# Splitting the normed tokens out of PSUM, and feeding a gated projection from stored high and low parts

## The chip, the cores and the metric

The kernel runs on one core of a Trainium2 chip. The metric is the device time in microseconds (us) of one execution. TensorE (PE in the profile; its weight loads are PEld) multiplies, VectorE (DVE), ScalarE (ACT) and GpSimd (POOL) work elementwise, and SyncE (SP) issues most of the DMAs. SBUF is the working memory of all engines; PSUM is where TensorE's results land.

## The reference

One layer of a hybrid decoder trunk, 2048 tokens of 1024 channels, all in float32. What is computed, cut to what matters here:

```
h  = rmsnorm(x, norm_pre_mix)                 # 2048 x 1024
z  = h @ w_in                                 # split into g_u, g_v | q, k, v, gate | q_mem
A  = gelu(g_u) * (tril(w_s) @ rmsnorm(gelu(g_v)) + b_s)      # spatial gating, chunks of 128 tokens, 6 groups
B  = forgetting attention over q, k, v, 6 heads x 64: softmax(q k / 8 + c[t] - c[s]) v
C  = attention of q_mem to 256 memory rows, 4 heads x 64
x  = x + rmsnorm(concat(A, B, C) @ w_out)
x  = x + rmsnorm(relu(rmsnorm(x) @ w_ff1)^2 @ w_ff2)         # 1024 -> 4096 -> 1024
```

## The kernel before

**Two parts for each number.** TensorE multiplies in a format with fewer bits than float32 (fp32r in the profile). So a number a is split into a high part (a copy or cast to fp32r) and a low part (a minus the high part), and a product is three matmuls: high by high, high by low, low by high (`mm3`, lines 201 to 203). Making the two parts costs one ACT or DVE cast and one DVE or POOL subtraction for each tile.

**Blocks and their sums.** Large products use seven products of 2 x 2 blocks in place of eight. For this the transposed normed tokens are wanted as four blocks (channels by halves, token tiles by pairs) and four sums t1 to t4 of the blocks, all of them in high and low parts.

**The stages**, in the order of the program:

- Rows stage 0 (`rows_stage(0, h)`, about 8 to 69 us): 1024 tokens, as four pairs of token tiles of 128 x 1024. For a tile: load x (line 409), the sum of squares by an ACT Square whose own output is not used ("junk", line 395), square root (207) and reciprocal (208), then one DVE operation `h = x * r * gain` (397), eight TensorE transposes into two PSUM banks (427). Each bank is one block of 128 x 512, called `pt`. Each block is copied by ACT to SBUF (`hb`, line 428), then split from there (`halves`, lines 400 and 401): high by ACT, low by DVE. Four DVE subtractions on `hb` give the sums (433 to 436), which are split too, with their low parts on POOL. One DMA of 1 MB stores `hb` of the pair to a DRAM scratch tensor `bq` (439). Then the projection to values and forget gates: 48 matmuls `va` per pair.
- Columns stage 0 (to about 149 us): queries and keys of these 1024 tokens, from the blocks and sums.
- Rows stage 1 and columns stage 1 for the other 1024 tokens (about 149 to 205, and 205 to 305 us). A tile scheduler sets the order of instructions in these four stages by its own estimates.
- Token mixing (about 305 to 842 us): the two attentions and the spatial gating with its projection `g_u, g_v`, interleaved. The order on every engine is written by a planner (`Plan`): it simulates the engines with a cost for each operation and with counts of free buffers, and takes the foremost ready operation by a due time `at`. For the gating, each of 16 token tiles is loaded back from `bq` into `hr` (line 1047, two buffers), split again into `ht` (ACT, line 1060; POOL, line 1063; two buffers) and multiplied as `ga`.
- Out-projection and the first feed-forward product, then the second feed-forward product (842 us to the end).

SP works its DMAs off in the order in which they stand in the program, and an issue that waits for something holds up those behind it. The PSUM pools of the first four stages are `ps_x` (4 banks), `ps_y` (2; used by the columns stages) and `ps_c` (2; the transposes). The normed tile `h` has one SBUF buffer for the first tile of a pair and one for the second (in pair 1 of stage 0 both tiles use the first). x tiles have two buffers.

Of the kernel before, what the change touches and what calls it, by code (L numbers as in the profile page):

```python
# [16 lines left out]
P = 128  # L17
S = 2048
D = 1024
# [21 lines left out]
def f32(ap):  # L41
    return ap.bitcast(F32)
# [9 lines left out]
class Plan:  # L52
    """Orders operations for engines that run in order: each engine in turn takes, of the operations whose inputs are
    there and whose buffers are free, the one that is foremost by 'at'. slots: how many buffers there are by name."""

    # until another engine sees a result
    SEEN = {"PE": 0.21, "ACT": 0.18, "DVE": 0.18, "Pool": 0.18, "SP": 0.1}
    # until the same engine does
# [71 lines left out]
def kernel(  # L130
# [46 lines left out]
    bq_d = [dram(f"bq{s}", [4, P, 4, KT // 2, P]) for s in range(NSB)]  # L177
# [40 lines left out]
    # Products of large matrices multiply 2 x 2 blocks by Winograd's seven products:  # L218
    # of blocks a11 .. a22 and b11 .. b22, with s and t sums of the blocks,
    #   c11 = p1 + p2, u2 = p1 + p6, u4 = u2 + p5, c12 = u4 + p3, c21 = u2 + p7 - p4, c22 = u4 + p7  # L220

    def combos(pl, src, nm, dst, q):
        """Blocks of 256 transposed tokens (channels by halves, tokens by tiles) and their sums, to dst"""
# [77 lines left out]
    def columns(nm, weights, h, kp, cp, px, py, emit, before):  # L301
        """Two column tiles of weights by 1024 tokens; emit(f, n, c): what becomes of columns f, tokens n"""
# [53 lines left out]
    # in-projection, 1024 tokens at a time: by rows the values and forget gates, by columns the queries and keys  # L356
# [26 lines left out]
    def rows_stage(s, h):  # L383
        """1024 tokens: norm, transposes, sums of blocks to h; values and forget gates"""
        with ExitStack() as st:
# [19 lines left out]
            def load_pair_of_tiles(q):  # L405
# [9 lines left out]
                # blocks b12, b11, b21, b22: channels by halves, tokens by tiles  # L415
                b = rp.tile([P, 4, KH, P], F32, name=f"hb{s}_{q}", tag="raw")
                own = [xc.tile([P, KH, P], F32R, name=f"b12{w}_{s}_{q}", tag=f"b12{w}") for w in range(2)]
                hl = {m: [t[:, q] for t in h[m]] for m in h}
                hl[0] = own
                for e, ms in enumerate(((1, 2), (0, 3))):  # L420
                    hn = (xd if e and s + q != 1 else xa).tile([P, D], F32, name=f"h{tiles[e]}", tag="h")
                    norm(tiles[e], xt[e], b[:, ms[0] : ms[1] + 1 : ms[1] - ms[0]].rearrange("p m k t -> p m (k t)"), hn)
                    for half, m in enumerate(ms):
                        pt = ps_c.tile([P, KH, P], F32, name=f"pt{s}_{q}_{m}", tag="c")
                        for k in range(KH):
                            kc = half * KH + k
                            nc.tensor.transpose(pt[:, k, :], hn[:, kc * P : (kc + 1) * P], ident)
                        (nc.scalar.copy if m in (0, 1, 2, 3) else nc.vector.tensor_copy)(b[:, m], pt)
                for m in (1, 2, 0, 3):
                    halves(m, hl[m], b[:, m])  # L430
                t1, t3, t2, t4 = [xb.tile([P, KH, P], F32, name=f"t{m}_{s}_{q}", tag="b") for m in (5, 7, 6, 4)]
                es = [nc.vector] * 4
                es[1].tensor_tensor(out=t3, in0=b[:, 3], in1=b[:, 0], op=ALU.subtract)
                es[0].tensor_tensor(out=t1, in0=b[:, 0], in1=b[:, 1], op=ALU.subtract)
                es[2].tensor_tensor(out=t2, in0=b[:, 3], in1=t1, op=ALU.subtract)
                es[3].tensor_tensor(out=t4, in0=b[:, 2], in1=t2, op=ALU.subtract)
                for m, t in ((7, t3), (6, t2), (4, t4), (5, t1)):
                    halves(m, hl[m], t)
                nc.sync.dma_start(bq_d[s][q], b)
                return tiles, hl  # L440

            def rows(tiles, hl):
                """Values and forget gates of two token tiles"""
# [17 lines left out]
    def forget_sums():  # L461
        """c_d: running sums of log sigmoid(gate)"""
        # log sigmoid(z) = min(z, 0) - log1p(exp(-|z|)), log1p(e) = 2 atanh(e / (2 + e))
# [41 lines left out]
    def out_sums(kk, sc):  # L505
        """Sums of the blocks of the out-projection's weights, rows kk of both halves"""
# [14 lines left out]
    def memory_keys(w1p, cp_):  # L521
        """Keys and values of the memory"""
# [48 lines left out]
    def gating_weights(hl, rows):  # L571
        """Of the spatial gating's projection the next rows"""
# [61 lines left out]
    def out_block(m, kk):  # L634
        """Rows kk of an operand of the out-projection's product m"""
# [8 lines left out]
    # token mixing  # L644
    with ExitStack() as st:
# [10 lines left out]
        # causal mask, as what is subtracted from a diagonal block of scores  # L656
# [8 lines left out]
        # weights of the spatial gating and of its projection; of the former the lower triangles, keys on partitions  # L665
# [16 lines left out]
        def chain(name, new):  # L682
            """Operations of one name start in the order in which they are given"""
# [4 lines left out]
        def load_pair(name, tag, hi, lo, half, cols):  # L688
            """[hi; lo] of 64 channels on 128 partitions"""
# [7 lines left out]
        def context(u, kt, half, b, pv, recip, at):  # L697
            """Sum of the halves of pv, over the row sums, to rows half*64.. of context tile kt"""
# [30 lines left out]
        def products(u, nk, first, source, values, vfree, pfree, deps, at):  # L729
            """Transposes the probabilities of 512 queries and multiplies them with the values; returns where the products are"""  # L730
# [864 lines left out]
```

## Time and profile before

| | us |
|---|---|
| runs | 2294.2, 2300.56, 2306.31 (median 2300.56) |
| profiled execution: span | 2300.8 |
| PE busy | 2179.4 (95%) |
| DVE busy | 1626.0 (71%) |
| ACT busy | 1356.0 (59%) |
| POOL busy | 1041.5 (45%) |

The profile's page states no time for the profiled execution other than its span, 2300.8 us from the first to the last instruction; that is the time the sums below are made against, and it lies 0.2 us from the median of the runs. In the profile a row of a group reads: line, engine, operation, result <- operands, shapes, count, then busy time, mean duration of one in ns, and the idle time of the engine just ahead of them with what ended it. A row of the timeline reads: start, duration, engine, line, operation. A row of a table of windows gives the busy time of each engine in a stretch of the span, the TensorE clock that was granted as a share of the full clock (PEclk), and the share of time and the rate of the DMA engines.

### The profile page before, as it was taken

The page shows a single profiled execution, that of the slowest core. Times are in us where ns is not written, and L with a number is a line of the kernel's source. Part 1 is how long each engine was busy: PE and PEld are TensorE (multiplying, and loading weights), DVE is VectorE, ACT ScalarE, POOL GpSimd, SP SyncE. Part 2 cuts the span into 40 slices and gives each one's busy share as a digit, 9 for nine tenths or more (in the row PEclk, how much of TensorE's full clock was granted, in tenths as well). Part 3 has the DMA queues.
Part 4 walks back from the last instruction along what each step waited for, and adds up shares of the span by engine and source line. Part 5 has one row for each costly group of instructions (what it writes and reads, how often), then busy time and mean ns, then how long its engine had stood idle before and what let it go on. Part 6 is the DMA issues. An engine that isn't in the chain of part 4 may idle for free. (4 is left out here: it accounts for less than half of the span.)

```text
span 2300.8 us, 33009 instructions
## 1 busy us (share of the span) xinstructions
PE 2179.4 (95%) x10468; PEld 1830.4 (80%) x10468; DVE 1626.0 (71%) x3137; ACT 1356.0 (59%) x2929; POOL 1041.5 (45%) x1073
## 2 busy tenths in 40 slices
PE   7999989999999979998999999999999999999996
PEld 7777768888888857776888878888788888888874
DVE  8779656777877798995333363333579988998899
ACT  6455567778877776675555575555654443344343
POOL 5445432362636155553333333353365435544564
PEclk9999999999999999999999999999999999999998
DMA  6775685365453355786333353343132212221245
GB/s 221 255 243 174 213 225 131 90 161 133 117 147 98 87 156 209 262 298 217 121 113 113 110 187 113 113 149 113 59 116 92 92 56 92 92 92 57 91 157 182
DMA packets 220715, 330.62 MB, mean 144 GB/s; under 512 B 23014, under 2 KB 139628, under 8 KB 219516
## 3 DMA queue, kind: packets, MB, share of 16 engines
q1 hardware_dynamic: 208252, 287.55, 40.2%
q0 software_dynamic: 12288, 40.95, 4.8%
q8 instruction: 83, 1.36, 0.2%
q14 instruction: 92, 0.75, 0.1%
HBM read 218.20 MB, written 110.23 MB: 143 GB/s over the span
## 5 line engine op out<-in xcount | busy, mean ns | idle before, releaser
L195 DVE TENSOR_TENSOR w_f<-sf,w_f 128x512 fp32r<-128x512 f32 x128 | 92.9, 726 | 176.0 <-ACT w_f L193 171.6
L201 PE MATMUL gx<-w,hc 128*128 128x512 f32 x512 | 200.0, 394 | 14.7 <-DVE ya L1478 11.1
L203 PE MATMUL fxf<-h,w_f 128*128 128x512 f32 x512 | 200.4, 391 | 6.4 <-DVE w_f L195 6.4
L202 PE MATMUL fxf<-h,w_f 128*128 128x512 f32 x512 | 200.0, 391 | 1.2 <-DVE h L195 1.2
L201 PE MATMUL fxf<-h,w_f 128*128 128x512 f32 x512 | 200.2, 391 | 0.9 <-ACT w_f L193 0.5
L202 PE MATMUL gx<-w,hc 128*128 128x512 f32 x512 | 200.3, 391 | 0.0
L193 ACT ACTIVATE hc<-hs 128x256 fp32r<-128x256 f32 x256 | 105.7, 414 | 156.2 <-PE gx L202 62.1
L203 PE MATMUL gx<-w,hc 128*128 128x512 f32 x512 | 196.8, 391 | 0.0
L748 DVE TENSOR_TENSOR pl<-pt,ph 128x512 fp32r<-128x512 f32 x240 | 140.8, 605 | 46.8 <-ACT ph L744 43.1
L195 DVE TENSOR_TENSOR hc<-hs,hc 128x256 fp32r<-128x256 f32 x256 | 146.9, 577 | 36.1 <-PE gx L203 33.8
L860 ACT ACTIVATE p<-p,nm 128x512 f32<-128x512 f32 (+2 forms) x240 | 156.9, 658 | 24.9 <-DVE nm L850 24.5
L1478 DVE TENSOR_TENSOR ya<-gx,ya 128x512 f32<-128x512 f32 x232 | 155.8, 678 | 4.6 <-PE gx L203 4.3
L744 ACT CAST ph<-pt 128x512 fp32r<-128x512 f32 x240 | 120.6, 523 | 63.8 <-PE pt L740 54.4
L193 ACT ACTIVATE hc<-hr 128x256 fp32r<-128x256 f32 x192 | 79.3, 416 | 126.8 <-PE gx L202 83.3
L195 DVE TENSOR_TENSOR w_f<-wrf,w_f 128x512 fp32r<-128x512 f32 x96 | 70.0, 729 | 110.8 <-ACT w_f L193 110.8
L193 ACT ACTIVATE w_f<-sf 128x512 fp32r<-128x512 f32 x128 | 80.8, 631 | 106.3 <-PE fxf L202 61.8
L831 DVE CUSTOM_DVE_ANT_0 p<-s,cb 128x512 f32<-128x512 f32 (+2 forms) x216 | 124.6, 592 | 18.5 <-PE pt L740 10.2
L1459 POOL TENSOR_TENSOR hs<-hr 128x256 f32<-128x256 f32 x64 | 59.6, 932 | 167.9 <-DVE hc L195 75.2
L201 PEld LDWEIGHTS gx<-w,hc 128*128 128x128 f32 x512 | 96.7, 189 | 38.5 <-DVE ya L1478 14.5
L740 PE MATMUL pt<-ident,p 128*128 128x128 f32 x816 | 124.1, 278 | 2.7 <-ACT p L860 2.6
L810 POOL TENSOR_TENSOR cm<-cb,cmask 128x128 f32<-128x128 f32 x96 | 44.9, 468 | 175.9 <-DVE mx L831 141.1
L740 PEld LDWEIGHTS pt<-ident,p 128*128 128x128 f32 x816 | 102.7, 144 | 23.2 <-ACT p L860 2.9
(380 smaller groups left out, 7089.6 us busy)
## 6 DMA issues: line engine op xcount, KB each, us to landing
wrf<-in_w_ff_dram SPq DMA_DIRECT2D x64, 512.0 KB, 4.8
hid<-c_f SPq DMA_DIRECT2D x128, 256.0 KB, 2.2
hr<-hid SPq DMA_DIRECT2D x64, 512.0 KB, 4.1
w2r<-in_w_ff_dram SPq DMA_DIRECT2D x16, 1024.0 KB, 6.6
b<-ty POOLq DMA_DIRECT2D x56, 256.0 KB, 3.7
xt<-in_x_dram SPq DMA_DIRECT2D x16, 512.0 KB, 4.1
bq<-hb SPq DMA_DIRECT2D x8, 1024.0 KB, 5.3
hr<-bq SPq DMA_DIRECT2D x32, 256.0 KB, 5.0
```

The costliest lines, as they stand in the source:

```text
L193: a = nc.scalar.activation(hi, src, AF.Copy, scale=scale)
L195: return a, (eng or nc.vector).tensor_tensor(out=lo, in0=src, in1=f32(hi), op=ALU.subtract)
L201: nc.tensor.matmul(acc, lh, rh, start=first, stop=False, skip_group_check=more)
L202: nc.tensor.matmul(acc, lh, rl, start=False, stop=False, skip_group_check=more)
L203: nc.tensor.matmul(acc, ll, rh, start=False, stop=last, skip_group_check=more)
L740: nc.tensor.transpose(pt[:, a * P : (a + 1) * P], source(a, j), ident)
L744: nc.scalar.copy(hi[:, a0 * P :], tiles["pt", j][:, a0 * P :])
L748: nc.vector.tensor_tensor(out=lo[:, a0 * P :], in0=tiles["pt", j][:, a0 * P :], in1=f32(tiles["hi", j][:, a0 * P :]), op=ALU.subtract,)
L831: nc.vector.tensor_tensor_reduce(out=pr[:, cols], in0=t["s", a, c][:, cols], in1=sub, scale=1.0, scalar=-3.0e38, op0=ALU.subtract, op1=ALU ...
L860: nc.scalar.activation(pr, pr, AF.Exp, bias=t["nm", a], accum_out=t["rs"][:, a, c : c + 1])
L1459: nc.gpsimd.tensor_tensor(out=t[7], in0=a11, in1=a21, op=ALU.subtract)
L1478: nc.vector.tensor_tensor(out=y, in0=a, in1=y, op=ALU.add)
```

## The change

In the rows stages:

- The blocks are split straight from the PSUM banks of the transposes: the high part (ACT) and the low part (DVE) read `pt`. Only blocks 0 and 1 are still copied to SBUF, as second operands of the sums; the sums' first operand is `pt`. So eight DVE operations of a pair that read two SBUF operands now read one PSUM and one SBUF operand, with t2's and t4's second operand still a sum in SBUF, and two of four ACT copies go.
- A bank is held until its last reader is done; the banks of the pair's second tile come from `ps_y`.
- The Square's unused output goes to `h` itself, no longer to `hb`.
- The DRAM scratch `bq` holds high and low parts in place of the values: eight stores of 256 KB for a pair in place of one of 1 MB.

In token mixing, a token tile's high and low parts are loaded ready, two loads of 512 KB in place of two of 256 KB, and the ACT cast and the POOL subtraction go. What the planner orders there is simulated anew, with these operations gone, and with the load of a tile waiting for one of two `ht` buffers (there were two `hr` buffers ahead of them).

```diff
-    bq_d = [dram(f"bq{s}", [4, P, 4, KT // 2, P]) for s in range(NSB)]
+    bq_d = [dram(f"bq{s}", [4, 2, 2, P, 2, KT // 2, P]) for s in range(NSB)]
...
-                b = rp.tile([P, 4, KH, P], F32, name=f"hb{s}_{q}", tag="raw")
+                b = rp.tile([P, 2, KH, P], F32, name=f"hb{s}_{q}", tag="raw")
...
+                pts = {}
                 for e, ms in enumerate(((1, 2), (0, 3))):
                     hn = (xd if e and s + q != 1 else xa).tile([P, D], F32, name=f"h{tiles[e]}", tag="h")
-                    norm(tiles[e], xt[e], b[:, ms[0] : ms[1] + 1 : ms[1] - ms[0]].rearrange("p m k t -> p m (k t)"), hn)
+                    norm(tiles[e], xt[e], hn.rearrange("p (m c) -> p m c", m=2), hn)
                     for half, m in enumerate(ms):
-                        pt = ps_c.tile([P, KH, P], F32, name=f"pt{s}_{q}_{m}", tag="c")
+                        bank, tag = (ps_y, "y") if e else (ps_c, "c")
+                        pt = pts[m] = bank.tile([P, KH, P], F32, name=f"pt{s}_{q}_{m}", tag=tag)
                         for k in range(KH):
                             kc = half * KH + k
                             nc.tensor.transpose(pt[:, k, :], hn[:, kc * P : (kc + 1) * P], ident)
-                        (nc.scalar.copy if m in (0, 1, 2, 3) else nc.vector.tensor_copy)(b[:, m], pt)
-                for m in (1, 2, 0, 3):
-                    halves(m, hl[m], b[:, m])
+                        if m in (0, 1):
+                            nc.scalar.copy(b[:, m], pt)
+                        halves(m, hl[m], pt)
+                        for w in range(2):
+                            nc.sync.dma_start(bq_d[s][q, e, w, :, half], f32(hl[m][w]))
...
-                es[1].tensor_tensor(out=t3, in0=b[:, 3], in1=b[:, 0], op=ALU.subtract)
-                es[0].tensor_tensor(out=t1, in0=b[:, 0], in1=b[:, 1], op=ALU.subtract)
-                es[2].tensor_tensor(out=t2, in0=b[:, 3], in1=t1, op=ALU.subtract)
-                es[3].tensor_tensor(out=t4, in0=b[:, 2], in1=t2, op=ALU.subtract)
+                nc.vector.tensor_tensor(out=t3, in0=pts[3], in1=b[:, 0], op=ALU.subtract)
+                nc.vector.tensor_tensor(out=t1, in0=pts[0], in1=b[:, 1], op=ALU.subtract)
+                nc.vector.tensor_tensor(out=t2, in0=pts[3], in1=t1, op=ALU.subtract)
+                nc.vector.tensor_tensor(out=t4, in0=pts[2], in1=t2, op=ALU.subtract)
...
-                nc.sync.dma_start(bq_d[s][q], b)
...
-                        t["hr", i] = xp.tile([P, D], F32, name=f"hr{i}", tag="x").rearrange("p (k t) -> p k t", k=KT)
-                        for k2 in range(2):
-                            nc.sync.dma_start(
-                                t["hr", i][:, k2 * KH : (k2 + 1) * KH], bq_d[s][q][:, ((1, 2), (0, 3))[e][k2]]
-                            )
...
-                    ld = chain("ld2", op("SP", 1.0, tokens, [], at - 8.0, takes=["hr"], late=4.0))
...
-                        o = chain("th", op("ACT", 0.478, thigh, [ld], at - 4.0, takes=["ht"] * (k2 == 0)))
-                        ht.append(op("Pool", 1.225, tlow, [o], at - 4.0, frees=["hr"] * k2))
+                        for w in range(2):
+                            t["ht", i, w] = hp.tile([P, KT, P], F32R, name=f"ht{w}_{i}", tag=f"ht{w}")
+                            load(
+                                t["ht", i, w].rearrange("p k t -> p (k t)"),
+                                bq_d[s][q, e, w].rearrange("p h k t -> p (h k t)"),
+                            )
+                    ht.append(chain("ld2", op("SP", 1.0, tokens, [], at - 8.0, takes=["ht"], late=4.0)))
```

Two places show how the change moves instructions. In the rows below `pt` are the transposes' banks, `hb` the SBUF copies of blocks, `hc` and `b` the high and low parts, `xt` the x tiles, `h` the normed tiles, `ss` the sums of squares, `r` the root, `vs` the values.

First place: ACT in rows stage 0 from the transposes of pair 1 on. Before:

```order
L428 COPY hb_1_330<-pt_1_1_340 128x512
L395 ACTIVATE hb_2_460,ss_464<-xt_456 128x1024
L428 COPY hb_1_330<-pt_1_2_346 128x512
L400 CAST hc_1_202<-hb_1_330 128x512
L207 ACTIVATE r<-ss_464,eps_t 128x1
L193 ACTIVATE vs_451<-va_426 128x6x64
L400 CAST hc_2_198<-hb_1_330 128x512
L428 COPY hb_1_330<-pt_1_0_359 128x512
L428 COPY hb_1_330<-pt_1_3_365 128x512
L400 CAST b_0_1_331<-hb_1_330 128x512
L395 ACTIVATE hb_2_460,ss_483<-xt_457 128x2x512
L400 CAST hc_3_190<-hb_1_330 128x512
```

And now:

```order
L431 COPY hb_1_335<-pt_1_1_345 128x512
L400 CAST hc_1_202<-pt_1_1_345 128x512
L400 CAST hc_2_198<-pt_1_2_355 128x512
L395 ACTIVATE h_364,ss_365<-xt_332 128x1024
L207 ACTIVATE r<-ss_365,eps_t 128x1
L193 ACTIVATE vs_566<-va_541 128x6x64
L431 COPY hb_1_335<-pt_1_0_371 128x512
L400 CAST b_0_1_336<-pt_1_0_371 128x512
L400 CAST hc_3_190<-pt_1_3_381 128x512
L395 ACTIVATE h_473,ss_474<-xt_466 128x1024
L395 ACTIVATE h_499,ss_500<-xt_467 128x1024
L207 ACTIVATE r<-ss_474,eps_t 128x1
```

Two copies are gone. The Squares of pair 2 (`xt_456` and `xt_457` before, `xt_466` and `xt_467` now) stood among the copies and casts of pair 1; now both stand behind pair 1's last cast, and the Square of pair 1's own second tile (`xt_332`) stands between the casts of the first and those of the second.

Second place: SP at the start of token mixing, down to the queries of the second block of 512 (`q_0_2`). `cb`, `q`, `k` and `v` belong to the forgetting attention, `gvn`, `gws` and `wur` are weights of the gating. Before:

```order
L797 DMA cb_0_3118<-c_d 128x512
L1047 DMA hr_3104<-bq_91 128x512 x2
L187 DMA v_0_3120<-v_d 128x4x128
L797 DMA cb_1_3125<-c_d 128x512
L187 DMA q_0_1_3107<-qhi_67 64x512 x2
L187 DMA q_0_1_3110<-qlo_70 64x512 x2
...
L187 DMA v_1_3127<-v_d 128x4x128
L985 DMA gvn<-in_gmlp_v_norm_dram 128x384
L984 DMA gws<-in_gmlp_w_s_dram 128x6x128
L187 DMA q_0_2_3156<-qhi_67 64x512 x2
L187 DMA q_0_2_3159<-qlo_70 64x512
```

And now:

```order
L187 DMA v_0_3161<-v_d 128x4x128
L799 DMA cb_1_3166<-c_d 128x512
L187 DMA v_1_3168<-v_d 128x4x128
L799 DMA cb_2_3277<-c_d 128x512
L187 DMA q_0_1_3148<-qhi_67 64x512 x2
...
L987 DMA gvn<-in_gmlp_v_norm_dram 128x384
L187 DMA q_0_2_3195<-qhi_67 64x512
L187 DMA ht_0_3144<-bq_91 128x1024
L187 DMA ht_0_3146<-bq_91 128x1024
L986 DMA gws<-in_gmlp_w_s_dram 128x6x128
L187 DMA q_0_2_3195<-qhi_67 64x512
```

The first token tile's load stood second in the stage and was 512 KB; now it is 1 MB and stands behind the first block's queries and keys, in the midst of the second block's queries, and one more `cb` stands ahead.

More of the change, by code (lines that the diff above doesn't have):

```diff
@@ L427, in load_pair_of_tiles @@
                             nc.tensor.transpose(pt[:, k, :], hn[:, kc * P : (kc + 1) * P], ident)
-                        (nc.scalar.copy if m in (0, 1, 2, 3) else nc.vector.tensor_copy)(b[:, m], pt)
-                for m in (1, 2, 0, 3):
-                    halves(m, hl[m], b[:, m])
-                t1, t3, t2, t4 = [xb.tile([P, KH, P], F32, name=f"t{m}_{s}_{q}", tag="b") for m in (5, 7, 6, 4)]
-                es = [nc.vector] * 4
-                es[1].tensor_tensor(out=t3, in0=b[:, 3], in1=b[:, 0], op=ALU.subtract)
-                es[0].tensor_tensor(out=t1, in0=b[:, 0], in1=b[:, 1], op=ALU.subtract)
-                es[2].tensor_tensor(out=t2, in0=b[:, 3], in1=t1, op=ALU.subtract)
-                es[3].tensor_tensor(out=t4, in0=b[:, 2], in1=t2, op=ALU.subtract)
+                        if m in (0, 1):
[3 more added lines that the diff above has]
+                            nc.sync.dma_start(bq_d[s][q, e, w, :, half], f32(hl[m][w]))
+                t1, t3, t2, t4 = [xb.tile([P, KH, P], F32, name=f"t{m}_{s}_{q}", tag="b") for m in (5, 7, 6, 4)]
+                nc.vector.tensor_tensor(out=t3, in0=pts[3], in1=b[:, 0], op=ALU.subtract)
+                nc.vector.tensor_tensor(out=t1, in0=pts[0], in1=b[:, 1], op=ALU.subtract)
+                nc.vector.tensor_tensor(out=t2, in0=pts[3], in1=t1, op=ALU.subtract)
+                nc.vector.tensor_tensor(out=t4, in0=pts[2], in1=t2, op=ALU.subtract)
                 for m, t in ((7, t3), (6, t2), (4, t4), (5, t1)):
                     halves(m, hl[m], t)
-                nc.sync.dma_start(bq_d[s][q], b)
                 return tiles, hl
@@ L1044, in tokens @@
                         s, e, q = i // 8, i // 4 % 2, i % 4
-                        t["hr", i] = xp.tile([P, D], F32, name=f"hr{i}", tag="x").rearrange("p (k t) -> p k t", k=KT)
-                        for k2 in range(2):
-                            nc.sync.dma_start(
-                                t["hr", i][:, k2 * KH : (k2 + 1) * KH], bq_d[s][q][:, ((1, 2), (0, 3))[e][k2]]
-                            )
-                    ld = chain("ld2", op("SP", 1.0, tokens, [], at - 8.0, takes=["hr"], late=4.0))
-                    for k2 in range(2):
-                        ks = slice(k2 * KH, (k2 + 1) * KH)
-                        def thigh(i=i, k2=k2, ks=ks):
-                            for w in range(2):
-                                t["ht", i, w, k2] = hp.tile(
-                                    [P, KH, P], F32R, name=f"ht{w}_{k2}_{i}", tag=f"ht{w}_{k2}"
-                                )
-                            nc.scalar.copy(t["ht", i, 0, k2], t["hr", i][:, ks])
-                        def tlow(i=i, k2=k2, ks=ks):
-                            nc.gpsimd.tensor_tensor(
-                                out=t["ht", i, 1, k2], in0=t["hr", i][:, ks], in1=f32(t["ht", i, 0, k2]), op=ALU.subtract
-                            )
-                        o = chain("th", op("ACT", 0.478, thigh, [ld], at - 4.0, takes=["ht"] * (k2 == 0)))
-                        ht.append(op("Pool", 1.225, tlow, [o], at - 4.0, frees=["hr"] * k2))
+                        for w in range(2):
[3 more added lines that the diff above has]
+                                bq_d[s][q, e, w].rearrange("p h k t -> p (h k t)"),
+                            )
+                    ht.append(chain("ld2", op("SP", 1.0, tokens, [], at - 8.0, takes=["ht"], late=4.0)))
                     for w in range(2):
@@ L1075, in project @@
                             mm3(
-                                t["ga", w][:, :DG], t["ht", i, 0, k // 4][:, k % 4, :], t["ht", i, 1, k // 4][:, k % 4, :],
+                                t["ga", w][:, :DG], t["ht", i, 0][:, k, :], t["ht", i, 1][:, k, :],
                                 wg[k][0][:, cs], wg[k][1][:, cs], k == 0, k == KT - 1,
```

## The prediction

> **What bounds the kernel now.** I read the table of windows first, to see which engine is full in which stage, then DVE's groups by shape in the stages that change, then what PE waits for there.
>
> ```profile
> 8.00:69.00 61.00, 51.98 (x256) 48.69 (x256) 57.29 (x77) 36.30 (x74) 36.53 (x24) 0.92 0.65 226
> 149.00:205.00 56.00, 46.57 (x250) 42.53 (x249) 48.92 (x72) 35.17 (x73) 30.19 (x21) 0.94 0.61 212
> 305.00:322.00 17.00, 9.64 (x35) 8.05 (x36) 7.91 (x30) 9.63 (x22) 8.01 (x16) 0.80 1.04 297
> 322.00:800.00 478.00, 461.40 (x2800) 414.91 (x2799) 351.71 (x1092) 373.49 (x960) 194.47 (x258) 0.99 0.49 123
> 800.00:842.00 42.00, 29.25 (x141) 20.79 (x140) 39.07 (x87) 34.30 (x73) 23.23 (x29) 0.88 0.37 113
> 240.00:250.00 10.00, 7.53 (x33) 5.75 (x32) 8.01 (x11) 5.47 (x10) 3.46 (x5) 0.84 1.01 310
> ```
>
> After start and end come the width, then PE, PEld, DVE, ACT and POOL busy, the granted clock, the DMA share and GB/s. In the two rows stages (first two rows) the fullest engine is DVE: 57.29 of 61 us (94%) and 48.92 of 56 (87%); ACT, at 36.30 and 35.17, is far from full. Token mixing's long middle belongs to PE (461.40 of 478). Its first 17 us belong to the DMAs (share 1.04), its last 42 to DVE (39.07). The last row is ten microseconds in which the DMA engines were full: 310 GB/s is their ceiling here. Behind 842 us the code is the same.
>
> **The rows stages: shorter DVE operations.** DVE's groups by shape, of stage 0 (three rows) and stage 1 (three rows):
>
> ```profile
> L401 DVE TENSOR_TENSOR hc<-hb,hc 128x512 fp32r<-128x512 f32 x12 | 16.2, 1359 | 0.5 <-ACT hc L400 0.5
> L436 DVE TENSOR_TENSOR t<-hb,t 128x512 f32<-128x512 f32 x4 | 6.0, 1508 | 0.0
> L401 DVE TENSOR_TENSOR b<-hb,b 128x512 fp32r<-128x512 f32 x4 | 2.7, 680 | 0.0
> ...
> L401 DVE TENSOR_TENSOR hc<-hb,hc 128x512 fp32r<-128x512 f32 x12 | 12.1, 1022 | 1.0 <-ACT hc L400 1.0
> L436 DVE TENSOR_TENSOR t<-hb,t 128x512 f32<-128x512 f32 x4 | 6.6, 1641 | 0.0
> L401 DVE TENSOR_TENSOR b<-hb,b 128x512 fp32r<-128x512 f32 x4 | 4.9, 1218 | 0.0
> ```
>
> One and the same form, 128x512 minus 128x512, costs 0.68 us in the third row and 1.0 to 1.6 in the others. What stretches it, and whether a PSUM operand takes that away, is told by another line (token mixing, `pt` in PSUM, `ph` in SBUF) and by a piece of the timeline:
>
> ```profile
> L748 DVE TENSOR_TENSOR pl<-pt,ph x240: 259/680/693, 327.5 to 842.5; 128x512 fp32r<-128x512 f32 x96, 128x256 fp32r<-128x256 f32 x24
> ...
> 831.81 2.41 POOL L1152 TENSOR_TENSOR gl<-z,gh 128x384 fp32r<-128x384 f32 x2
> 832.32 1.28 DVE L748 TENSOR_TENSOR pl<-pt,ph 128x512 fp32r<-128x512 f32 x2
> 833.52 1.25 DVE L963 TENSOR_TENSOR wo<-wor,wo 128x512 fp32r<-128x512 f32 x1
> ```
>
> Of 240 operations with one operand in PSUM the longest took 0.693 us (columns: least, median, most), and two of them ran at 0.64 apiece while POOL worked. The next, with two SBUF operands, took 1.25 under the same POOL work. So reading `pt` should bring the lows and most sums to 0.68. That saves in stage 0: lows 12 x (1.359 - 0.680) = 8.1, and the last sum 4 x (1.508 - 0.680) = 3.3, at most 11.4 us; in stage 1: 12 x (1.022 - 0.680) = 4.1, 4 x (1.218 - 0.680) = 2.2, 4 x (1.641 - 0.680) = 3.8, at most 10.1. The two copies of a pair that go are ACT's, under whose slack they lie; they are worth a shorter chain and nothing in busy time.
>
> The stages can't shorten by all of that, since two other things are close behind. First **PE**:
>
> ```profile
> PE pt L427 <- DVE h L397: 12.6, 4, 8.0
> PE va L203 <- DVE b L401: 2.0, 1, 2.0
> PE va L203 <- DVE hc L401: 1.0, 1, 1.0
> ...
> 66.11 0.34 PE L202 MATMUL va<-wv,hc 128*128 128x390 f32 x1
> 144.80 1.03 PE L427 MATMUL pt<-ident,h 128*128 128x128 f32 x8
> ```
>
> In stage 0 PE waits for DVE 15.6 us in all, 8.0 of them for the first tile, which stays; that leaves 7.6. A pair's 48 value products at about half of the 0.34 they show (they overlap in pairs), and 16 transposes at 1.03 for eight, are about 8.4 + 2.1 us; with about 1.5 for restarts, 12 us against the 61 / 4 = 15.2 and 56 / 4 = 14.0 of now. Second the **DMAs**:
>
> ```profile
> xt<-in_x_dram SPq DMA_DIRECT2D x16, 512.0 KB, 4.1
> bq<-hb SPq DMA_DIRECT2D x8, 1024.0 KB, 5.3
> v_d<-vs SPq DMA_DIRECT2D x16, 384.0 KB, 2.4
> ```
>
> A pair moves now two `xt`, one `bq`, two `v_d`, 2816 KB; then 3840 KB, or 3.93 MB. At 310 GB/s that is 12.7 us a pair, below the present 15.2 and 14.0 by 2.5 and 1.3. So the gain ends at about 4 x 2.5 = 10 us in stage 0 (PE's waits say 7.6, so 8) and 4 x 1.3 = 5 in stage 1, and at 0 if stores and loads don't fit between one another. Near the ceiling they will in part hold x back; I take about half of each: **-4.5 and -3.5**, bounds 0 to -8 and 0 to -5.
>
> **The new waits in the rows stages.** The Square's unused output is now `h`, so it must wait until the transposes have read the tile before in that buffer. Its chain:
>
> ```profile
> L395 ACT ACTIVATE hb<-xt 128x1024 f32<-128x1024 f32 x8 | 8.5, 1059 | 4.7 <-DMA xt<-in_x_dram 4.7
> L207 ACT ACTIVATE r<-ss,eps_t 128x1 f32<-128x1 f32 x8 | 2.4, 296 | 0.1
> L397 DVE SCALAR_TENSOR_TENSOR h<-xt,r,gain_pre 128x1024 f32<-128x1024 f32 x7 | 10.8, 1542 | 0.1
> ```
>
> Square 1.06, root 0.30, about 0.3 for the sum's read and the reciprocal, and 1.54 for `h`: 3.2 us, and 1.0 of transposes make 4.2 for a tile. First and second tile have their own buffers except in pair 1, so a pair's loop is 4.2 to 8.4, under 12: no charge, +1 as the bound. Behind a waiting Square on ACT stand the root, and the `vs` evictions (L193), which free PE's banks; in the order shown it comes behind all of pair 1's casts, so nothing of pair 1 waits. Banks held until t2 and t4 have read them: t4 stands ahead of the next pair's `h` on DVE, so the bank is free before new transposes can start: 0, +1 as the bound.
>
> **The start of token mixing.**
>
> ```profile
> 308.21 0.67 PE L820 MATMUL s<-k,q 128*128 128x512 f32 x1 [3.45 <-DMA k<-klo]
> 319.71 0.77 PE L821 MATMUL s<-k,q 128*128 128x512 f32 x1 [4.15 <-DMA q<-qlo]
> ```
>
> Here PE waits for bytes. Ahead of the second block's low queries 512 KB are added by the larger first token tile, and 256 KB by one more `cb`: 0.79 MB at 310 GB/s, 2.5 us. The first queries and keys, on the other hand, no longer stand behind the 512 KB token tile (1.7 us), and six more gating products fill part of the second wait. I take **+1**, bounds 0 and +2.5.
>
> **The middle.** What goes from ACT and POOL there:
>
> ```profile
> L1060 ACT CAST ht<-hr 128x512 fp32r<-128x512 f32 x32 | 19.0, 627 | 0.1
> L1063 POOL TENSOR_TENSOR ht<-hr,ht x32: 1265/1288/1302, 307.9 to 743.1; 128x512 fp32r<-128x512 f32 x32
> PE pv L761 <- POOL ph L755: 5.9, 4, 2.3
> PE sm L907 <- DMA q_m<-mhi: 3.1, 4, 1.6
> PE sm L908 <- DMA q_m<-mlo: 2.2, 4, 0.9
> PE s L821 <- DMA q<-qlo: 1.7, 4, 0.6
> ...
> 646.56 1.51 POOL L715 TENSOR_TENSOR ctm<-ctm,crm 64x512 f32<-64x512 f32 x1 [2.11 <-DMA crm<-r_d]
> ```
>
> 19.0 us of ACT and 32 x 1.29 = 41 of POOL, under a PE that is busy 97%. PE's largest wait, 5.9 us for `ph` on POOL, comes where POOL itself sits behind `crm`, a DMA (last row), so it is not the subtractions' doing. 8 MB more traffic at a mean share of 0.49 fits; the 7.0 us of waits for `q` and `q_m` in these rows can grow or shrink. **0**, bounds -3 and +3.
>
> **The tail, 800 to 842.** DVE is its limit, and its products and weight splits stay. The new order on PE leaves, behind the last gating product, 78 transposes, 52 `pv` and 24 `s` products, where 62, 44 and 18 stood; that fills a stage in which PE has 13 us idle, at the price of nothing that ran earlier. I take **-1**, bounds 0 and -3.
>
> **The sum.** -4.5 - 3.5 + 1 + 0 - 1 = -8. Against the profiled execution's span of 2300.8 us, 0.2 above the runs' median, that gives 2292.8, so 2293.
>
> **The rivals.**
>
> *Small stores move slower* (slower). Eight 256 KB stores, in 2 KB pieces to DRAM, replace one of 1 MB. If the queue then only carries the stages' present mean rates, 226 and 212 GB/s, a pair takes 3.93 / 0.226 = 17.4 and 18.5 us: 4 x (17.4 - 15.2) + 4 x (18.5 - 14.0) = +27, about 2327. It decides from the rate at which 3.93 MB no longer fit: 259 GB/s in stage 0, 281 in stage 1. Against it: the shares of 0.65 and 0.61 say that the engines were idle a third of that time, and 512 KB and 384 KB transfers filled the queue at 310 GB/s. For it: SP issues in order, and eight stores that each wait for a high or low part now stand ahead of the x loads. The Trainium skill has a rule that speaks against this edit (DMA: Bandwidth & Descriptors, section Bandwidth): batch transfers to at least 1 MiB to get 75% of the peak; it states 341 GB/s at 1 MB and 138 at 64 KB, with no row at 256 KB. By an estimate from those two figures a store would move somewhere between; the trace shows 310 GB/s with mixed sizes down to 256 KB, so it bears the rule out only in part.
>
> *Nothing that can be told* (about 2300). DVE gets shorter, but x comes late by as much: the Square waits 4.7 us for `xt` already, and 1 MB more stands before each pair's loads, 1024 KB / 310 GB/s = 3.4 us a pair or 27 us in all if none of it were hidden. A quarter of that unhidden, 7 us, cancels the 8.
>
> *More* (about 2281). Both stages reach their floors, -8 and -5, the copies' absence shortens the first pair, and the tail gives 3, with +1 at the start of mixing at most -4 more from steadier clock: where PE paused in these stages its clock was granted at 0.92 and 0.94. -8 - 5 - 3 - 4 + 1 = -19, about 2282.
>
> *The lows don't shorten* would need PSUM operands to suffer under POOL too; the 693 ns above leave it no more than the weight already in the second rival.
>
> **How the numbers follow.** Forecast 0.55, with its own range 2286 to 2300; small stores 0.10; nothing 0.18; more 0.17. A measurement of this kernel tells about 0.5%, 11.5 us, from no change: faster is below 2289.1, slower above 2312.1. Of the forecast, a third lies below 2289 (0.18), the rest within; of "more", all but a little is faster (0.16); of "nothing", 0.02 is faster and 0.01 slower; the small stores are slower (0.10). Faster 0.36, same 0.53, slower 0.11. The range reaches from "more", 2279, to 2308: past "nothing" plus the start's and the waits' upper bounds, but not to 2327.
>
> **What would show it.** Right: `hc` lows at 0.68 in both stages; DVE's busy time there down by about 11 and 10 us; the stages' ends (first product of the columns) 4 to 5 and 8 earlier; PE's waits for `h` and lows smaller, and in their place waits for `xt`; token mixing as long as before within 3 us. Wrong: lows above 1 us though `pt` is read; `xt` landing later than the Square could start, by more than 2 us a pair; DMA rates in the stages below 280 GB/s with a share near 1; PE waiting for `ht` in the middle; or a Square that waits for transposes and holds `vs` evictions behind it.

## The result: slower by 1.0%, and where in the kernel

The changed kernel takes 2322.7 us (median of four runs, 2321.1 to 2325.0) against 2301.2 us for the kernel before (2294.2 to 2306.3): a ratio of 1.0102, with a 95% interval of 1.0084 to 1.0120. The prediction was 2293 us in a range of 2279 to 2308, so it missed the sign as well as the range. The profiled execution has a span of 2319.4 us.

The same four marks in each trace show in which part the time went. They are the starts of the first `pv` product (token mixing has got under way), of the last `ga` product (the gating's projection is done), and of the first `fxf` product (the first feed-forward product has begun), and the end of the span. The rows below are differences of starts that the trace gives for these tiles. The experiments, told further down, stand in the same table. Medians are of the timed runs; the sections are of one profiled execution each, which lies up to 9 us off its kernel's median. The experiments ran on four chips, on which the kernel before took 2300.0 to 2302.4 us in the median: ratios are to the kernel before on the same chip, and a difference between medians of two chips is good to some 2 us.

| kernel | first `pv` at | to the last `ga` | to the first `fxf` | to the end | span | median |
|---|---|---|---|---|---|---|
| before | 328.4 | 472.1 | 219.0 | 1281.3 | 2300.8 | 2301.2 |
| changed | 318.9 | 484.3 | 232.1 | 1284.1 | 2319.4 | 2322.7 |
| e1: rows part alone | 318.4 | 468.7 | 221.9 | 1282.5 | 2291.5 | 2290.8 |
| e2: stored parts alone | 326.1 | 488.3 | 233.7 | 1284.1 | 2332.2 | 2334.1 |
| e3: changed, old order | 321.8 | 476.1 | 224.3 | 1279.9 | 2302.1 | 2308.8 |
| e11: e3 again | 322.3 | 477.9 | 223.4 | 1279.6 | 2303.2 | one run, 2305.0 |
| e4: changed, three `gch` | 320.9 | 477.2 | 233.6 | 1283.5 | 2315.2 | 2307.8 |
| e12: e4 again | 324.2 | 471.3 | 229.9 | 1285.1 | 2310.5 | one run, 2312.2 |
| e5: e3, half the bytes | 319.3 | 471.0 | 223.6 | 1281.0 | 2294.9 | 2293.7 |
| e9: changed, half the bytes | 321.3 | 476.3 | 233.5 | 1282.4 | 2313.5 | 2315.9 |
| e6: e4, gating due later | 317.8 | 481.6 | 223.2 | 1278.8 | 2301.4 | 2305.4 |
| e7: e1, gating due later | 316.7 | 511.3 | 204.3 | 1279.5 | 2311.8 | 2305.2 |
| e8: e1, due times stretched | 317.8 | 483.9 | 222.6 | 1280.4 | 2304.7 | 2310.8 |
| e10: e1, SBUF operands | 330.6 | 469.7 | 220.1 | 1281.0 | 2301.4 | 2300.5 |

Between before and after, the four columns give -9.5, +12.2, +13.1 and +2.8 us, in sum the 18.6 us by which the spans differ. So the rows stages did gain what was forecast. Token mixing lost more than twice that.

### The profile page after: what moved, and what is told of

The parts are those of the page before. It is cut to its first block, busy times and chain, and to the rows that moved or that the text cites. A ratio compares the mean times of both kernels' runs of the same rounds, so it can differ in the third digit from the quotient of the medians.

```text
span 2319.4 us, 33068 instructions
## 1 busy us (share of the span) xinstructions
PE 2187.4 (94%) x10468; PEld 1835.2 (79%) x10468; DVE 1606.5 (69%) x3137; ACT 1332.5 (57%) x2881; POOL 999.1 (43%) x1041
## 5 line engine op out<-in xcount | busy, mean ns | idle before, releaser
L201 PE MATMUL fxf<-h,w_f 128*128 128x512 f32 x512 | 200.1, 391 | 0.9 <-ACT w_f L193 0.5
```

What stands on the lines that cost most here:

```text
L201: nc.tensor.matmul(acc, lh, rh, start=first, stop=False, skip_group_check=more)
```

## The profile after

First the table of windows of the changed kernel (start and end; width; PE, PEld, DVE, ACT and POOL busy; granted clock; DMA share; GB/s): the two rows stages, token mixing up to the last `ga` product, and the tail behind it.

```profile
8.00:64.00 56.00, 48.61 (x257) 45.23 (x258) 48.39 (x79) 32.21 (x67) 33.66 (x24) 0.97 0.87 299
142.00:195.00 53.00, 48.50 (x264) 45.28 (x262) 43.66 (x74) 32.53 (x68) 28.63 (x23) 0.94 0.89 312
319.00:803.00 484.00, 457.22 (x2745) 412.80 (x2744) 344.58 (x1064) 352.74 (x911) 154.62 (x224) 0.97 0.51 135
803.00:860.00 57.00, 41.37 (x189) 30.19 (x188) 46.39 (x114) 41.05 (x87) 27.35 (x34) 0.79 0.32 93
```

In the rows stages DVE has fallen from 57.29 and 48.92 us busy to 48.39 and 43.66, and the DMA engines are busy 87% and 89% of the time, at 299 and 312 GB/s: the doubled stores do fit. In mixing POOL has fallen as it should, and PE gained nothing by it. In the tail the granted clock is 0.79 where it was 0.88.

DVE's groups by shape in rows stage 0 of the changed kernel:

```profile
L397 DVE SCALAR_TENSOR_TENSOR h<-xt,r,gain_pre 128x1024 f32<-128x1024 f32 x7 | 13.1, 1877 | 0.1
L401 DVE TENSOR_TENSOR hc<-pt,hc 128x512 fp32r<-128x512 f32 x12 | 7.9, 681 | 0.6 <-ACT hc L400 0.6
L439 DVE TENSOR_TENSOR t<-pt,t 128x512 f32<-128x512 f32 x4 | 2.7, 680 | 0.0
```

The lows cost 0.681 us in place of 1.359, the last sum 0.680 in place of 1.508. A part of it is given back: `h`, which still reads two SBUF operands, went from 1.54 to 1.88 us, probably because POOL's work now falls on it more often; no run tests that.

What PE waited for in token mixing of the changed kernel (total, times, longest), the two rows that grew most, and one that is new:

```profile
PE ga L201 <- ACT gch L1187: 10.0, 2, 5.7
PE pt L742 <- ACT p L862: 6.3, 3, 4.9
...
PE ga L201 <- DMA ht<-bq: 4.6, 1, 4.6
```

The same waits before:

```profile
PE pt L740 <- ACT p L860: 2.6, 1, 2.6
...
PE gpt L1195 <- ACT gch L1201: 1.2, 1, 1.2
```

The first row of the changed kernel is the largest wait of the stage; before, PE waited 1.2 us for `gch`, ahead of a `gpt` transpose. The wait for `p` lies almost whole in the tail (5.9 us of it), that for `ht` at the first token tile, ahead of the first `pv`. The timelines of the changed kernel around its first occurrence, ACT's, SP's and PE's:

```profile
478.17 0.59 ACT L1187 COPY gch<-gpt 128x512 f32<-128x512 f32 x1
488.38 0.58 ACT L1187 COPY gch<-gpt 128x512 f32<-128x512 f32 x1 [6.58 <-DMA ctx<-gch]
...
479.62 1.58 SPq L935 DMA_DIRECT2D r_d<-rim  x2
483.24 0.45 SPq L187 DMA_DIRECT2D mk<-km  x1
484.30 0.37 SPq L1190 DMA_DIRECT2D ctx<-gch  x1
...
489.01 0.69 PE L201 MATMUL ga<-wua,ht 128*128 128x384 f32 x1 [4.29 <-ACT gch L1187]
```

The gating's result is turned by PE into a bank, copied by ACT to the one `gch` buffer, and stored by SP. The first copy ends at 478.8, but SP, which issues in order, comes to its store only at 484.30. The second copy waits for that store to land; it holds a bank of the gating's two; and the next `ga` product, which needs the bank, holds PE. What held SP in these microseconds, from its own waits between 478 and 485 us:

```profile
SPq L187 <- DMA ht<-bq: 2.0, 1, 2.0
SPq L935 <- DMA ht<-bq: 0.9, 1, 0.9
SPq L1190 <- DMA v<-v_d: 0.5, 1, 0.5
SPq L935 <- DMA cb<-c_d: 0.3, 1, 0.3
```

Of these 3.7 us, 2.9 are put down to loads of token tiles, now 1 MB for each tile. What PE loses is more than the wait, as four-microsecond windows of the changed kernel show:

```profile
481.00:485.00 4.00, 3.73 (x24) 3.07 (x23) 2.34 (x8) 0.80 (x2) 0.46 (x1) 1.00 0.77 162
485.00:489.00 4.00, 0.00 (x0) 0.00 (x0) 0.14 (x2) 0.62 (x2) 0.00 (x0) 0.74 0.62 160
489.00:493.00 4.00, 3.99 (x12) 3.80 (x13) 2.30 (x8) 2.98 (x8) 0.41 (x1) 0.50 0.26 74
493.00:497.00 4.00, 4.00 (x23) 3.53 (x22) 2.54 (x10) 2.41 (x7) 0.51 (x2) 0.91 0.67 181
```

Behind 4 us in which PE did nothing, it did 12 products in the next 4 us, at a granted clock of 0.50, where the windows on either side hold 24 and 23. So a stall of 4.3 us cost some 6.3, as 4 us at half the clock lose 2. The second stall, of 5.7 us, is followed by the same 0.50 (751 to 755 us). The Trainium skill (TensorE: Matmul & The Clock Gate, section Part 1: The HAM clock gate) states that after about 3.4 us of idleness the clock is halved, for about as long; this trace agrees, with 0.50 for about 4 us behind 4.3 us and behind 5.7 us.

## The experiments

**e1, the rows part alone.** Against the kernel before:

```diff
-                        pt = ps_c.tile([P, KH, P], F32, name=f"pt{s}_{q}_{m}", tag="c")
+                        bank, tag = (ps_y, "y") if e else (ps_c, "c")
+                        pt = pts[m] = bank.tile([P, KH, P], F32, name=f"pt{s}_{q}_{m}", tag=tag)
...
-                for m in (1, 2, 0, 3):
-                    halves(m, hl[m], b[:, m])
+                        halves(m, hl[m], pt)
...
-                es[1].tensor_tensor(out=t3, in0=b[:, 3], in1=b[:, 0], op=ALU.subtract)
+                es[1].tensor_tensor(out=t3, in0=pts[3], in1=b[:, 0], op=ALU.subtract)
```

(and so for the other three sums). Expected:

> The kernel before with the rows part of the change alone: lows and sums read the transposes' PSUM banks, the banks of the second tile come from ps_y; all four blocks are still copied to SBUF by ACT, the Square writes to the copy's buffer, the store is 1 MB of values a pair, and token mixing is as before. Theory A (the rows stages gain, token mixing's new order loses): the first pv product starts 7 to 10 us earlier than before (328.4 us there, 318.9 in the changed kernel), mixing keeps its 516 us from the first pv to the first ox product, and the whole takes 2301 - 8 = 2291 to 2295 us. Theory B (the rows gain comes from the copies and the 1 MB store that go, not from PSUM operands): first pv after 325 us, 2298 us or more.

It took 2290.8 us (2286.7 to 2293.2), a ratio of 0.9955 to before, 0.9942 to 0.9968. The first `pv` is at 318.4, and from there to the first `ox` product it takes 513.9 us. Theory A holds, and B falls: the gain is there with all four copies and the 1 MB store in place. This kernel beats both; of all that were run it is the fastest.

**e10, which half of the rows part.** e1 with its lows and sums reading the copies again (`halves(m, hl[m], b[:, m])`, and `b[:, m]` for `pts[m]` in the sums), the banks as in e1.

> The kernel of e1 with one thing undone: the lows and the sums read the blocks' copies in SBUF again, while the second tile's banks still come from ps_y and a block is split right after its copy. If the rows gain of e1 (9.6 us) is DVE's shorter operations on PSUM operands, it goes: lows back at 1.0 to 1.4 us in the mean, first pv at 325 to 330 us, 2298 to 2303 us. If it is the two more banks (transposes that wait for no reader): lows long, yet first pv near 319 and 2291 to 2294 us.

2300.5 us, a ratio of 0.9998 (0.9988 to 1.0008): the whole gain is gone. DVE's lows and last sum in its rows stage 0:

```profile
L401 DVE TENSOR_TENSOR hc<-hb,hc 128x512 fp32r<-128x512 f32 x12 | 16.1, 1358 | 0.5 <-ACT hc L400 0.5
L436 DVE TENSOR_TENSOR t<-hb,t 128x512 f32<-128x512 f32 x4 | 6.0, 1506 | 0.0
```

These are the durations of before (1359 and 1508 ns). By their edits e1 and e10 differ in nothing but where the casts, the subtractions and the sums read a block. ACT's casts of the blocks take as long either way (625 and 626 ns in rows stage 0), so the 9.7 us are shown to come from where DVE reads one operand. The first `pv` is at 330.6, a little over what was expected.

**e2, the stored parts alone.** The changed kernel with the rows part taken back: four copies, everything read from SBUF, two banks, and the eight stores and the changed gating kept.

> The changed kernel with the rows part undone: four copies, lows and sums read SBUF, one pair of PSUM banks, the Square's output in the copy's buffer; high and low parts are stored in eight pieces of 256 KB and the gating is fed from them, with the changed order. Theory A: mixing takes 540 us from the first pv to the first ox product as in the changed kernel, the rows stages are as before to +4 us, so 2301 + 24 to 2301 + 30 = 2325 to 2331 us. If the rows part's new reads were what upset token mixing (Theory C), mixing would be back near 516 us and the time near 2301.

2334.1 us (2331.7 to 2337.7), a little over what was expected, a ratio of 1.0151 to before (1.0138 to 1.0164). The sections show why theory C falls: mixing takes 488.3 and 233.7 us, as in the changed kernel. And the rows stages are no longer than before for eight small stores: the first product of the columns is at 69.3 us in both, the last value product at 200.1 for 203.7.

**e3, the stored parts in the old order.** In the changed kernel the planner is told of operations that issue nothing, so that it orders everything else as before; the third buffer lies where `hr` was:

```diff
-                    ht.append(chain("ld2", op("SP", 1.0, tokens, [], at - 8.0, takes=["ht"], late=4.0)))
+                    ld = chain("ld2", op("SP", 1.0, tokens, [], at - 8.0, takes=["hr"], late=4.0))
+                    for k2 in range(2):
+                        o = chain("th", op("ACT", 0.478, lambda: None, [ld], at - 4.0, takes=["ht"] * (k2 == 0)))
+                        ht.append(op("Pool", 1.225, lambda: None, [o], at - 4.0, frees=["hr"] * k2))
```

> The changed kernel, but the planner still counts the ACT cast and the POOL subtraction of each half token tile and the two hr buffers, with nothing issued for them: so PE, DVE, ACT and POOL keep the order of the kernel before in token mixing. A third buffer for a token tile's parts lies where hr was, since loads are issued earlier in that order. The bytes are those of the changed kernel. Theory A (the order): first pv at about 319 us, mixing 516 to 521 us, the two waits of ga for gch (10.0 us) gone, the tail behind the last gating product 44 us instead of 56; 2292 to 2297 us. Theory D (8 MB more traffic and loads of 1 MB for a tile delay queries, keys and stores whatever the order): mixing stays over 528 us, 2304 us or more.

2308.8 us (2303.8 to 2312.2), 1.0038 times before (1.0025 to 1.0052). The time is theory D's; the 521.3 us from the first `pv` to the first `ox` are at the edge of theory A's. The order gives 13.9 us of the loss back (2322.7 - 2308.8), the tail with it (224.3 us for 232.1), and the waits for `gch` fall to 1.3 us. Yet it is still 18.0 us over e1, which has the same order on PE, DVE, ACT and POOL, and the cast and the subtraction on top. (SP's loads of token tiles stand earlier in e3 than in e1.) So theory A alone isn't enough.

**e5, half the bytes in the old order.** e3 with `[:, :KH]` of each part loaded and `k % KH` multiplied.

> The kernel of e3 (stored parts, the order of before), but of each token tile only the first half of the channels' high and low parts is loaded, and the gating's products use it for both halves: left out is half of the gating's input, so its output is another; the instructions on PE, DVE, ACT and POOL are the same in number and order, the bytes loaded for the gating are those of the kernel before (8 MB, not 16). Theory D' (what is left between e1, 2291, and e3, 2309, is the 8 MB more of loads: queries and keys come later, and each longer wait is followed by a slower clock): first pv to first ox back from 521 us to 513 to 516, waits of s and sm for q, k and q_m back from 19 us to 15 or less, 2291 to 2296 us. Theory E (it is the eight stores a pair, the order on SP or the third buffer): 519 us or more, 2301 to 2309 us.

2293.7 us (2287.5 to 2299.1 in eleven runs), 0.9965 times before (0.9953 to 0.9978). Of e3's 18.0 us over e1, 15.1 go with the 8 MB of loads: e5 keeps e3's third buffer, its eight stores and its order on SP, so theory E falls. D' holds by the time, and at its edge by the 516.2 us from the first `pv` to the first `ox`. PE's waits that a DMA ended, summed over token mixing, are 14.6 us in e5, against 19.0 in e3, 20.0 in its second profile (e11) and 15.1 in e1. The waits of SP on the landing of token tiles in mixing, from the views of four kernels, in this order: before, changed, e3, e5.

```profile
SPq L187 <- DMA hr<-bq: 1.8, 3, 0.9
SPq L719 <- DMA hr<-bq: 0.7, 1, 0.7
SPq L797 <- DMA hr<-bq: 0.6, 1, 0.6
SPq L1204 <- DMA hr<-bq: 0.5, 1, 0.5
```

```profile
SPq L187 <- DMA ht<-bq: 4.4, 4, 2.0
SPq L935 <- DMA ht<-bq: 3.3, 3, 1.4
SPq L799 <- DMA ht<-bq: 2.3, 2, 1.3
SPq L1190 <- DMA ht<-bq: 1.7, 1, 1.7
```

```profile
SPq L187 <- DMA ht<-bq: 7.5, 5, 2.0
SPq L935 <- DMA ht<-bq: 2.4, 2, 1.8
```

```profile
SPq L187 <- DMA ht<-bq: 0.2, 1, 0.2
```

3.6, 11.7, 9.9 and 0.2 us (12.6 in e11). By these rows SP stands behind loads that haven't landed, and what follows in its order is late, though the DMA engines are busy only half the time (a share of 0.51 above). In the profiles the difference between e3 and e5 is 7 to 8 us, 3 at the first `pv` and 5 to 7 up to the last `ga`, both in the first profile of e3 and in the second (e11); the medians say 15. So the cost of the bytes is shown, and PE's longer waits for DMAs are 4 to 5 us of it; what the typical run loses beyond that can't be seen in these profiles, and stays open.

> The kernel of e3 once more, for a second profile: its first one is of an execution 5 us under the median of its runs, so that the stages of e3 and e5 don't differ by as much as the medians. If the bytes cost in the middle of token mixing, first pv to last ga is 478 to 484 us here against 471 in e5; the rest as in e5 to 3 us. If the difference lies behind token mixing: first pv to last ga 476 or less, and the feed-forward part longer than e5's.

477.9 us from first `pv` to last `ga`, just under what was expected for the middle, against 471.0 in e5; behind it the two agree within 1.6 us.

**e4, three buffers for `gch`.** The changed kernel in its own order; the second and third copy of a group go to buffers that stood empty:

```diff
-                        t["gch", b, kt] = gp.tile([P, 4, P], F32, name=f"gch{b}_{kt}", tag="gch", bufs=1)
+                        t["gch", b, kt] = (
+                            xp.tile([P, 4, P], F32, name=f"gch{b}_{kt}", tag="x")
+                            if kt and b < 3 else gp.tile([P, 4, P], F32, name=f"gch{b}_{kt}", tag="gch", bufs=1)
+                        )
```

> The changed kernel with its order unchanged, and two more buffers for gch (the copies of the turned gating results on their way to DRAM) for three of the four groups of chunks: a copy no longer waits for the store of the one before, which stands on SP behind stores that wait for other results. Theory A1 (10 of the 24 us lost in mixing are the two waits of ga for gch, 4.3 and 5.7 us, and the slow clock behind them): these waits fall below 1 us in all, the last ga product starts about 10 us earlier than 802.8, the tail behind it stays at 56 us, 2309 to 2313 us. If the wait only moves to another resource (a bank, SP's queue): 2318 us or more.

2307.8 us (2306.0 to 2316.9), 14.9 under the changed kernel and a little better than expected. No `ga` product waits for `gch` any more, first `pv` to last `ga` falls from 484.3 to 477.2, and the tail keeps its length (233.6). So the two waits and the slow clock behind them are shown to have cost some 7 us by this profile, 13 by the next and 15 by the medians.

> The kernel of e4 once more, for a second profile: its first one is of an execution 9 us over the median of its runs. First pv to last ga should be 470 to 476 us (477.2 in the first), the tail behind it as long as in the changed kernel (232 us from the last ga to the first fxf product), the time 2306 to 2311 us. If the tail is at 224, the order's price for the tail isn't a fixed one.

A second profile, at 2312.2 us a little over what was expected: 471.3 us to the last `ga`, as expected, but a start that is 5 us later than the changed kernel's, where the first `ga` product waits 6.4 us for its tile; the tail is 229.9. Sections of one kernel move by up to 6 us from one execution to the next.

**e9, half the bytes in the changed order.**

> The changed kernel in its own order, with only the first half of the channels' high and low parts loaded for the gating's products and used for both halves (half of the gating's input is left out, as in e5). If the bytes and the order cost apart from each other: 2322.7 - 15 = 2306 to 2310 us, the two waits of ga for gch still there (8 to 10 us). If the two waits for gch come from the bytes too (stores late because SP's queue is long): they fall below 3 us and the time to 2292 to 2300. If bytes cost nothing in this order: 2320 us or more.

2315.9 us (2312.5 to 2317.6), 6.8 under the changed kernel (9 by the two ratios, 1.0063 and 1.0102): none of the three cases. The wait row of this kernel:

```profile
PE ga L201 <- ACT gch L1187: 4.6, 2, 3.8
```

With half the bytes the waits for `gch` are 4.6 us in place of 10.0, so by one profile of each the bytes made about half of them and the order the rest. The two causes don't add up as separate terms: the 8 MB cost 15.1 us in the old order and 6.8 in the changed one; the changed order costs 13.9 us with all the bytes and 22.2 with half (2315.9 - 2293.7).

**e6, e7 and e8, other due times for the gating.** These ask whether the tail's 13 us are the attention that is left behind the last `ga` product. In e6 and e7 `gating(4.0, ...)` becomes `gating(14.0, ...)`; in e8 the rate `1.41 * at` becomes `1.43 * at`.

> The kernel of e4 (changed kernel, three gch buffers), with the planner's due times of the gating 10 us later (they begin at 14 instead of 4 us of the stage): behind the last gating product then stand 42 transposes, 24 pv and no s products, where the changed kernel has 78, 52 and 24. Theory A2 (the tail's 12 us are the attention that the new order leaves behind the last gating product): from the last ga to the first ox 40 us or less instead of 55.5, and 2293 to 2301 us against 2308 for e4. If the tail is set by the gating's own chain or by the splits of the out-projection's weights on DVE: 50 us or more, 2304 us or more.

> The kernel of e1 (rows part alone, values stored) with the same later due times: no product of the attention is left behind the last gating product (62 transposes, 44 pv and 18 s in e1). Theory A2: the tail falls from 45 us to about 30 (the splits of the out-projection's weights are 14 us of DVE, and the gating's last chain runs beside them), PE carries 5 us more ahead of it, so 2278 to 2286 us, under e1's 2291. If PE has nothing to fill the gating's last chain with, the tail stays at 40 or more and the time at 2290 or above.

> The kernel of e1 (rows part alone) with the gating's due times stretched by 1.4 per cent (a factor of 1.43 for 1.41), so that they begin as before and end later: behind the last gating product stand 42 transposes and 26 pv products instead of 62, 44 and 18 s. If the attention left there costs its latency: from the last ga to the first fxf product 8 to 12 us less than e1's 221.9, at 3 to 5 us more ahead of it, so 2283 to 2288 us, under e1's 2291. If the work only changes places, as in e6 and e7: 2291 us or more.

e6 takes 2305.4 us (2302.5 to 2312.9), above theory A2's range and within that of the case against it; e7 2305.2 (2301.7 to 2313.6) and e8 2310.8 (2306.5 to 2327.2), both slower than e1 by 14 and 20 us. In e6 the way from the last `ga` to the first `ox` product shrank to 26.7 us, but part of that only moved: PE then waits inside the out-projection, as its waits show.

```profile
PE ox L201 <- ACT cx L193: 3.7, 1, 3.7
PE oy L202 <- DVE wo L195: 2.9, 2, 2.1
PE ox L203 <- DVE cx L195: 2.8, 1, 2.8
```

Of these, 6.5 us are for the high and low parts of the concatenated results (`cx`) and 2.9 for those of the out-projection's weights (`wo`). Up to the first `fxf` the tail is 223.2 us, 10 under e4's first profile and 7 under its second; e8, with as little attention left, has 222.6, no less than e1's 221.9, which has the old amount. So leaving more than the old order did cost 7 to 10 us, and leaving less gained nothing in e8. In e7, which leaves none, the tail is 18 us shorter than e1's. But what was moved ahead of the last `ga` was paid there: 15 us in e8 and 43 in e7, where the gating's first product starts 25 us later (327.6 for 303.1). Theory A2 holds for the direction of the tail in the changed kernel, and fails as a way to a faster one.

## Why the prediction was wrong, step by step

**DVE's operations in the rows stages: right in the mechanism and the time, not in the reason for taking half.** -4.5 and -3.5 us were forecast. The first product of the columns came at 63.8 in place of 69.3 (-5.5), and the last value product at 194.7 in place of 203.7 (-9.0, so -3.5 for the second stage). The lows came to 0.68 us as forecast, and e10 shows that it was the operand in PSUM. DVE's busy time fell by 8.9 and 5.3 us and not by about 11 and 10, in part because `h` took longer. The forecast halved the possible gain because the DMAs, near a ceiling of 310 GB/s, would hold x back. But the changed kernel moved 312 GB/s at a share of 0.89, so 310 was no ceiling; and e1, e7 and e8, which store 1 MB a pair as before, have their first product of the columns at 62.6 to 63.1 us and their last value product at 192.4 to 194.8, so by these marks the doubled stores cost the changed kernel 2.3 us at the most. That half was so close was luck, and what held back the rest of the gain isn't shown.

**The new waits in the rows stages: right at nothing.** In stage 0 PE waits 11.3 us for `h` instead of 12.6, and no row there names the Square or a bank held too long; in stage 1 one row of 0.3 us has the transposes wait for a bank's cast.

**Small stores: rightly given a small chance, wrongly made the only slower case.** 256 KB stores ran in stages that moved 299 and 312 GB/s, and e2's rows stages were not longer. The Trainium skill's rule of 1 MiB (DMA: Bandwidth & Descriptors, section Bandwidth) asks for larger ones; no loss by it shows here.

**The start of mixing: +1 forecast, about 0 measured.** The columns end 9.3 us earlier (the last `fxc` at 295.1 for 304.4) and the first `pv` comes 9.5 earlier. In the old order the bytes may count at this place: e3's two profiles are 2.5 and 3.0 us later than e5's. But e4's two differ by 3.3 among themselves, so that isn't shown.

**The middle: 0 within 3 either way forecast, +12.2 measured.** This step failed. "8 MB more traffic at a mean share of 0.49 fits" took a mean over 478 us for the state of the queue at each moment. e5 shows that the 8 MB cost 15.1 us in the old order all the same, with SP's waits for token tiles at 9.9 us where half the bytes leave 0.2. That a query or a store then comes too late on an in-order SP is seen at the `gch` store above; how much of the 15 us goes that way is open. And the step looked for what was removed, and never priced what the new order put in SP's queue ahead of a store for which there was one buffer: the 3.7 us that ACT waited for `gch` before were in the trace, in four waits that cost PE 1.2.

**The tail: -1 forecast, +13.1 measured.** This step failed in its sign. The counts of products behind the last gating product (78, 52 and 24 for 62, 44 and 18) were right, and their reading was not. I took them to fill PE's idle 13 us. DVE set that stretch, as the prediction itself had said (39.07 of 42 us busy), and the products brought DVE and ACT work with them: DVE is busy for 46.39 us of 57 in the changed tail, with PE waiting on ACT and DVE between. The longest of the waits there, 4.9 us for `p`, was 2.6 before. e3, with the old counts, takes back 7.8 us of the 13.1 (8.7 in its second profile), and e6, with fewer, 8.9; the rest of the 13.1 isn't accounted for. That the products lengthen a chain over PE, ACT and DVE fits these rows, and is argued from them.

**The rivals.** None of them was a worse order. That the planner simulates the whole stage anew was in the text on the change, and it should have been a rival with a price on either side.

**Feed-forward.** Its code didn't change, and it took 2.8 us more. Across the kernels above it takes 1278.8 to 1285.1 us, and no run here was made to tell why.

In sum: rows -9.6 (e1, by medians), the stored parts +18.0 in the old order (of which 15.1 the bytes), and the changed order +13.9, from 2300.4 (the kernel before, beside e1) to 2322.7.

## What to carry to other kernels

When a change takes operations out of a list-scheduled stage, price the new schedule as a change of its own, and freeze the old order with operations that issue nothing to tell the two apart. A hidden operation that is replaced by bytes isn't free while DMA engines are half idle, if one queue issues everything in order: look at what that queue waits for, and for what has only one buffer behind it. And where DVE subtracts two SBUF operands beside a busy POOL, read one from PSUM if it is there.

## What was not expected of the hardware and the schedule

A single constant of the due times, moved by 1.4%, cost 20 us in the median (e8 against e1) with no operation added or removed; of the orders tried in token mixing beside the old one, none was clearly better at the same bytes: e7 and e8 were 14 and 20 us over e1, the changed kernel 14 over e3, and e4 and e6 within 3.4 us of e3. SP's waits on token tiles went from 3.6 to 9.9 us (12.6 in a second profile) when their size doubled and PE, DVE, ACT and POOL kept their order, at a mean DMA share of about a half. And a PE that stood still for 4.3 us, and once for 5.7, ran its next 4 us at a granted clock of 0.50, which makes a stall of 4 us half as dear again.
